# One-column products behind the spread of a root, AV beside the following transposes, and embedding copies behind the weight casts

## The chip, the cores and the metric

The kernel runs on one core of a Trainium2 chip. The core has a matmul engine (TensorE, PE in the profile, with its weight loads shown apart as PEld), three engines for elementwise work (VectorE = DVE, ScalarE = ACT, GpSimd = POOL) and a queue engine that issues DMAs (SyncE = SP). Matmul results land in PSUM, which has eight banks; all else lies in SBUF. The metric is the device time of one execution in microseconds.

## The reference, cut to what matters

A two-layer encoder trunk over 256 positions, width 2048, all in float32:

```python
for i in range(2):
    hn = rmsnorm(h, norm_g[i])
    a_val, a_glu, a_z, q, k, v, b_z = split(hn @ w_in[i])
    ya = conformer_conv(a_val, a_glu, ...)          # GLU, 31 taps, LayerNorm over channels, SiLU
    ya = ya * silu(a_z)
    yb = window_attention(q, k, v, bias, sink) * silu(b_z)   # 16 heads of 64, 4 key heads
    h = h + concat([ya, yb]) @ w_out[i]
    e = rmsnorm(p[i] @ w_pe[i], pe_g[i])
    h = h + e * sigmoid(h @ w_pg[i])
out = rmsnorm(h, final_g)
```

## The kernel before

Activations lie transposed, channels on the 128 partitions and the 256 positions along the free axis. Every large product is made of three fp32r matmuls of 256 columns (`mm3`, lines 399 to 401): the high part of the weights with the high and the low part of the activations, then the low part of the weights with the high part of the activations. Weights come by DMA in chunks of two halves of 128 x 1024. Each half is cast to its high part by ACT (L168), and DVE subtracts to get the low part (L171; L176 for the first two halves of layer 0). `ahead(h)` issues these splits up to half `h`, and a small pool of five split halves is kept in front of PE.

The order on DVE, PE and ACT is the order of the program text; only POOL's and SP's instructions are placed by the framework. Work beside the main stream is written as generators in a list `side`. `pump()` runs after every weight half (24 matmuls) and advances each generator in the list by one `yield`, in the order in which they were added; `wait(n)` yields n times. The depthwise convolution's taps (DVE, L559) are handed out by the same pump.

The parts that the change touches:

- `rstd_col` (L349) sums squares over channels with one-column products against a tile of ones (L354), each appearing as two PE records, then DVE scales (L359) and POOL raises to the power -0.5 (L361). `rstd_row` (L364) spreads that root over all partitions with two PE transposes of a broadcast column (L368), and ACT copies the row out (L372) unless `copy=False`. There are such pairs for the layer's input norm (`rh0`, `rh1`), for the embedding norm (`re0`, `re1`, in `embed`), for the convolution's LayerNorm (`rv0`, `rv1`, in `lnorm`, where `LY` gives the pumps waited before the sum and before the spread) and for the final norm (`rf`).
- A layer's first products are those of the embedding e = p @ w_pe: eight banks of two tiles each, indexed by `j // 2` (L473 to L509; plain float32 products at L481 in layer 0, `mm3` in layer 1). Among them stand the input norm's sum (at `j // 2 == QQ[l][0]`) and spread (at `QQ[l][1]`), the first splits of the input projection's weights, and the first normalised operands: `operand` multiplies by gain and root on DVE (L453, tile `hn`), ACT casts the high part (L456, tile `hg`) and DVE subtracts the low part (L457). The banks of e are copied out by ACT (L509); in layer 0 the first four wait until `j // 2` is 3, in layer 1 each is copied at once. The first input projection (tiles `ag`) follows, at first two weight halves interleaved.
- `attention` is one generator for each of eight pairs of heads (`i` from 0 to 7): scores on PE (L627, tile `sc`), softmax on DVE and ACT, eight transpose records on PE (L654, tile `pt`), two ACT copies (L658, tile `ptt`), then `wait(2)`, the product with v on PE (L664, tile `av`, eight records of 64 output partitions) and a DVE product with the gate (L667). In steady state one pair starts every four pumps, so PE sees: transposes of one pair, three halves of the projection, AV of that pair with the scores of the pair two later, one half, transposes of the next pair.

The output projection runs its attention half first (`o<-yb`), then its convolution half (`o<-ya`), then the gate product (`g<-h`).

Of the kernel before, what the change touches and what calls it, by code (L numbers as in the profile page):

```python
# [50 lines left out]
NSPL = 5  # L51
SHIFT = 16
MAN = 'DVE,PE,Activation'
LY = (2, 1)
ORD = 1
AW = (0,0,0,0)
NWARM = 6
# [72 lines left out]
def trunk_kernel(ctx: ExitStack, tc: tile.TileContext, xT, pT, wst, par, gain, relb, sinkp, onehot, out):  # L130
    nc = tc.nc
# [105 lines left out]
    def wait(n):  # L237
        for _ in range(n):
            yield
# [66 lines left out]
    ones = cst.tile([P, P], F32, name="ones")  # L306
# [54 lines left out]
        nc.gpsimd.tensor_tensor(col, v, mhalf, ALU.pow)  # L361
        return col

    def rstd_row(col, name, tag="rb", copy=True):  # L364

        bb = bank(name + "b")
        for b in range(2):
            nc.tensor.transpose(bb[:, 0, b * P:(b + 1) * P], col[:, b:b + 1].broadcast_to([P, P]), ident)  # L368
        if not copy:
            return bb[:, 0, :]  # L370
        rb = wk.tile([P, S], F32, name=name + "rb", tag=tag, bufs=1)
        nc.scalar.copy(rb, bb[:, 0, :])  # L372
        return rb

    def fold(a):
        t = wk.tile([P, S], F32, name="fold", tag="sg")
        nc.vector.tensor_add(t, a[:, 0, :], a[:, 1, :])
        return t

    def halves_of(a):  # L380
        return [a[:, 0, :], a[:, 1, :]]
# [54 lines left out]
    hacc = wk.tile([P, 2, S], F32, name="hacc", tag="hacc")  # L436
    for l in range(DEPTH):

        e = halves(bigt(f"e{l}"))
# [23 lines left out]
                    subs.pop(0)()  # L463

        ecopy = []
        for q in range(4):
            n = Cursor.h
            Cursor.h += 1
            if l:
                w = get(n).rearrange("p t (j k c) -> p t j k c", j=4, k=2)  # L470
            else:
                raw = raws[n // 2][:, n % 2, :].rearrange("p (j k c) -> p j k c", j=4, k=2)
            for jj in range(0, 4, 2):  # L473
                j = 4 * q + jj
                b = bank("e")
                for x in range(2):
                    for k in range(2):
                        if l:
                            mm3(b[:, x, :], w[:, :, jj + x, k, :], pp[:, :, k, :], x == 0 and k == 0, k == 1)
                        else:  # L480
                            nc.tensor.matmul(b[:, x, :], raw[:, jj + x, k, :], pf[:, k, :], start=x == 0 and k == 0,  # L481
                                             stop=k == 1, skip_group_check=True)
                if l == 0 and j // 2 < 4:
                    for k in (4 * (j // 2), 4 * (j // 2) + 2):
                        if k < KT - 2:
                            square_acc(hacc, h[k // 8][:, k % 8:k % 8 + 2, :], k == 0, nc.vector)
                    if j // 2 == 3:
                        sq = wk.tile([P, 2, S], F32, name="sq", tag="sq", bufs=3)
                        nc.scalar.activation(sq, h[1][:, 6:8, :], AF.Square)
                        hparts = [fold(hacc)] + halves_of(sq)  # L490
                if j // 2 == QQ[l][0]:
                    dg = rstd_col(hparts, D, f"rh{l}")
                    ahead(4 if l == 0 else Cursor.h - 1 - q + 5)
                if j // 2 == QQ[l][1]:
                    rbs.append(rstd_row(dg, f"rh{l}", copy=False))
                    if l == 0:
                        first_lo(4)
                        ahead(5)
                        operands(0, 1)
                        first_lo(5)  # L500
                        subs.pop(0)()
                        operands(2, 1)
                if QQ[l][1] + (l == 0) <= j // 2 <= QQ[l][1] + 1:
                    operands(4 * (j // 2 - QQ[l][1]), 2)
                ecopy.append((j, b))

                while ecopy and (l or j // 2 >= 3):
                    jc, bc = ecopy.pop(0)
                    nc.scalar.copy(e[jc // 8][:, jc % 8:jc % 8 + 2, :], bc)  # L509
            pump()  # L510
        subs.pop(0)()
        ahead(Cursor.h + 3)
        hsrc = xT if l == 0 else hscr

        def embed(l=l, eacc=eacc, e=e):

            if l == 0:
                yield from wait(8)
                bias_prep()
            for j in range(0, KT, 2):  # L520
                yield from wait(2)
                square_acc(eacc, e[j // 8][:, j % 8:j % 8 + 2, :], j == 0)
            yield from wait(6)
            es = fold(eacc)
            yield from wait(3)
            dg = rstd_col([es], D, f"re{l}")
            yield from wait(2)
            eb = rstd_row(dg, f"re{l}", "reb")
            yield from wait(50)
            while not state["enorm"]:  # L530
                yield
            for j in range(KT):
                d = e[j // 8][:, j % 8, :]
                nc.vector.scalar_tensor_tensor(d, d, pcol(l, PO_PE + j), eb, ALU.mult, ALU.mult)
                yield
# [52 lines left out]
        b = pair(hg, f"k{l}")  # L588
# [23 lines left out]
        def attention(i, qq, after, l=l, v=v, zb=zb):  # L612
            t = i // 4
            yield from wait(after)
            bias = load_bias(i)
            yield
            nm = wk.tile([P, 2, 2], F32, name="nm", tag="nm")
            den = wk.tile([P, 2, 2], F32, name="den", tag="den")
            es = wk.tile([P, 2, 2], F32, name="es", tag="es")
            sk = sinkt[:, l * NQ + 2 * i:l * NQ + 2 * i + 2].unsqueeze(1).broadcast_to([P, 2, 2])  # L620
            each = [(b, hh) for b in range(2) for hh in range(2)]
            o = []
            for b in range(2):
                o.append(bank("sc"))
                for hh in range(2):
                    for x in range(2):
                        nc.tensor.matmul(o[b][:, hh, :], qq[:, hh, b * P:(b + 1) * P], keys[t][x][:, hh, :],  # L627
                                         start=hh == 0 and x == 0, stop=x == 1, skip_group_check=True)
            yield from wait(1 + AW[0])
            s = [wk.tile([P, 2, S], F32, name="s", tag="s", bufs=4) for b in range(2)]  # L630
            for b, hh in each:
                c = l * NQ + 2 * i + hh
                nc.vector.tensor_tensor_reduce(
                    out=s[b][:, hh, :], in0=o[b][:, hh, :], in1=backwards(bias[:, hh, b * P:b * P + S]),
                    scale=1.0, scalar=nsink[:, c:c + 1], op0=ALU.add, op1=ALU.min,
                    accum_out=nm[:, b, hh:hh + 1])
            nc.vector.tensor_add(es, nm, sk)
            yield
            for b, hh in each:
                nc.scalar.activation(s[b][:, hh, :], s[b][:, hh, :], AF.Exp, bias=nm[:, b, hh:hh + 1],  # L640
                                     scale=-1.0, accum_out=den[:, b, hh:hh + 1])
            nc.scalar.activation(es, es, AF.Exp)
            yield from wait(1 + AW[1])
            nc.vector.tensor_add(den, den, es)
            nc.vector.reciprocal(den, den)
            yield from wait(1 + AW[2])
            for b, hh in each:
                nc.scalar.activation(s[b][:, hh, :], s[b][:, hh, :], AF.Copy, scale=den[:, b, hh:hh + 1])
            yield from wait(1 + AW[3])
            o = [bank("pt") for hh in range(2)]  # L650
            for hh in range(2):
                for b in range(2):
                    for kt in range(2):
                        nc.tensor.transpose(o[hh][:, kt, b * P:(b + 1) * P], s[b][:, hh, kt * P:(kt + 1) * P], ident)  # L654
            yield
            pt = [wk.tile([P, 2, S], F32, name="ptt", tag="ptt") for hh in range(2)]
            for hh in range(2):
                nc.scalar.copy(pt[hh], o[hh])  # L658
            yield from wait(2)
            o = bank("av")  # L660
            for kt in range(2):
                for hh in range(2):
                    g = 2 * t + hh
                    nc.tensor.matmul(o[hh * HD:(hh + 1) * HD, 0, :], v[:, kt, g * HD:(g + 1) * HD], pt[hh][:, kt, :],  # L664
                                     start=(kt == 0), stop=(kt == 1))
            yield
            nc.vector.tensor_mul(zb[:, i, :], o[:, 0, :], zb[:, i, :])  # L667
# [31 lines left out]
        def lnorm(l=l, acc=acc, za=za, ya=ya, ysum=ysum, done=done):  # L699
# [15 lines left out]
            yield from wait(LY[0])  # L715
            dg = rstd_col(halves_of(vacc), W_CONV, f"rv{l}")
            yield from wait(LY[1])
            rb = rstd_row(dg, f"rv{l}")
            yield
            for n in range(5):  # L720
                if n < 4:
# [202 lines left out]
```

## Time and profile before

| | us |
|---|---|
| median of three runs | 951.17 |
| lowest and highest run | 944.24, 951.45 |
| the profiled execution | 950.28 |
| its span, first to last instruction | 948.5 |
| PE busy in it | 935.5 (99%) |
| DVE busy | 769.4 (81%) |
| ACT busy | 549.4 (58%) |
| POOL busy | 83.8 (9%) |

The profile is of one execution. Times in it are microseconds from the start of its span. A row of the timeline has the start, the busy time, engine, line, operation and output<-inputs; a bracket at its end gives the engine's idle time before it and what ended that. A row of the windows gives, for a stretch of the span, the busy time and the number of records of each engine that overlap the stretch, the granted PE clock as a share of full speed, the share of the DMA engines in use and the rate in GB/s. PE records overlap, because matmuls are pipelined: the time that a matmul takes from its engine is the distance from its start to the next one's start, not its busy time. DMA moved 192 GB/s on average.

### The profile page before, as it was taken

Reading aid. Unit: us, or ns where it says so; the run is one execution under the profiler, and the core shown is the slowest. Engines: PE = TensorE matmul, PEld = TensorE weight load, DVE = VectorE, ACT = ScalarE, POOL = GpSimd, SP = SyncE. Lnnn points to the kernel's source line nnn. Section 1 sums busy time; section 2 is a strip of 40 time slices with the busy share of each in tenths; the row PEclk is TensorE's granted clock in tenths of the full one; section 3 lists DMA queues with packets and bytes.
Section 4 is the critical chain, followed back from the end, with each engine's and each line's share of the span. In section 5 each row is a group of like instructions: output and inputs, shape, how many; then the busy total and the mean of one; then the engine's idle time right before and its main releaser. Section 6 shows DMA issues by size and latency. Waiting matters only on the chain.

```text
span 948.5 us, 19102 instructions
## 1 busy us (share of the span) xinstructions
PE 935.5 (99%) x7952; PEld 918.8 (97%) x7952; DVE 769.4 (81%) x1290; ACT 549.4 (58%) x830; POOL 83.8 (9%) x79
## 2 busy tenths in 40 slices
PE   8999999999999999999999999999999999999995
PEld 7999999999999999999999999999999999999995
DVE  3899999998887676776679998999888878677663
ACT  4655455787875554454466444558787555546551
POOL 0022001010000000011103200000100010000111
PEclk9999999999999999999999999999999999999998
DMA  8674556555456465556555566465454564655532
GB/s 294 226 254 157 200 178 244 195 188 191 168 174 231 171 224 183 178 179 225 189 196 198 174 219 206 154 217 199 167 205 144 190 223 146 246 186 178 191 121 90
DMA packets 29011, 182.55 MB, mean 192 GB/s; under 512 B 3595, under 2 KB 4156, under 8 KB 9084
## 3 DMA queue, kind: packets, MB, share of 16 engines
q1 hardware_dynamic: 24284, 165.70, 49.9%
q0 software_dynamic: 3344, 12.88, 4.2%
q10 hardware_dynamic: 1296, 2.75, 0.8%
q8 instruction: 62, 1.02, 0.4%
q14 instruction: 25, 0.20, 0.1%
HBM read 177.09 MB, written 4.23 MB: 191 GB/s over the span
## 4 chain that ended last, share of the span: by engine, by line
PE 95%; DVE 3%; DMA 1%; issue 0%; ACT 0%; POOL 0%; ACTq 0%; DVEq 0%
PE g L401 6%; PE g L399 6%; PE g L400 6%; PE ag L401 6%; PE ag L399 6%; PE ag L400 6%; PE o L400 6%; PE o L399 6%; PE o L401 6%; PE za L399 3%; PE zb L400 3%; PE za L400 3%; PE zb L401 3%; PE zb L399 3%; PE q L399 3%; PE za L401 3%
## 5 line engine op out<-in xcount | busy, mean ns | idle before, releaser
L171 DVE TENSOR_TENSOR w<-raw,w 128x1024 fp32r<-128x1024 f32 x306 | 373.2, 1228 | 105.1 <-ACT w L168 104.5
L168 ACT CAST w<-raw 128x1024 fp32r<-128x1024 f32 x308 | 316.2, 1046 | 166.3 <-PE ag L401 40.6
L559 DVE SCALAR_TENSOR_TENSOR cz<-az,pars,cz 128x241 f32<-128x241 f32 (+11 forms) x480 | 217.8, 502 | 1.0
L401 PE MATMUL ag<-hg,w 128*128 128x256 f32 x512 | 143.0, 279 | 0.6 <-DVE w L171 0.5
L399 PE MATMUL ag<-hg,w 128*128 128x256 f32 x512 | 142.8, 279 | 0.0
L401 PE MATMUL g<-h,w 128*128 128x256 f32 x512 | 142.6, 279 | 0.0
L399 PE MATMUL g<-h,w 128*128 128x256 f32 x512 | 142.6, 278 | 0.0
L400 PE MATMUL g<-h,w 128*128 128x256 f32 x512 | 142.6, 278 | 0.0
L400 PE MATMUL ag<-hg,w 128*128 128x256 f32 x512 | 142.5, 278 | 0.0
L401 PEld LDWEIGHTS ag<-hg,w 128*128 128x128 f32 x512 | 96.2, 188 | 1.2 <-DVE w L171 1.0
L401 PEld LDWEIGHTS g<-h,w 128*128 128x128 f32 x512 | 97.2, 190 | 0.0
L400 PEld LDWEIGHTS ag<-hg,w 128*128 128x128 f32 x512 | 96.9, 189 | 0.1
L399 PEld LDWEIGHTS ag<-hg,w 128*128 128x128 f32 x512 | 96.1, 188 | 0.9 <-ACT w L168 0.8
L399 PEld LDWEIGHTS g<-h,w 128*128 128x128 f32 x512 | 96.1, 188 | 0.0
L400 PEld LDWEIGHTS g<-h,w 128*128 128x128 f32 x512 | 96.1, 188 | 0.0
L399 PE MATMUL o<-yb,w 128*128 128x256 f32 x256 | 72.2, 282 | 0.0
L399 PE MATMUL za<-hg,w 128*128 128x256 f32 x256 | 72.0, 281 | 0.0
L400 PE MATMUL o<-yb,w 128*128 128x256 f32 x256 | 71.6, 280 | 0.0
L399 PE MATMUL q<-hg,w 128*128 128x256 f32 x256 | 71.5, 279 | 0.0
L401 PE MATMUL o<-yb,w 128*128 128x256 f32 x256 | 71.4, 279 | 0.0
L399 PE MATMUL zb<-hg,w 128*128 128x256 f32 x256 | 71.4, 279 | 0.0
L399 PE MATMUL o<-ya,w 128*128 128x256 f32 x256 | 71.3, 278 | 0.0
(219 smaller groups left out, 2269.4 us busy)
## 6 DMA issues: line engine op xcount, KB each, us to landing
raw<-in_wst SPq DMA_DIRECT2D x153, 1024.0 KB, 4.9
bias<-fscr POOLq DMA_DIRECT2D x16, 384.0 KB, 4.0
raw<-in_wst SPq DMA_DIRECT2D x4, 512.0 KB, 8.0
az<-in_xT POOLq DMA_DIRECT2D x4, 512.0 KB, 5.3
hscr<-e POOLq DMA_DIRECT2D x2, 1024.0 KB, 5.5
az<-hscr POOLq DMA_DIRECT2D x4, 512.0 KB, 5.8
x<-in_xT SPq DMA_DIRECT2D x3, 512.0 KB, 8.2
out_t<-og ACTq DMA_DIRECT2D x4, 256.0 KB, 3.0
```

The lines of the kernel that those rows point to most:

```text
L168: nc.scalar.copy(hi, raw)
L171: nc.vector.tensor_sub(lo, raw, hi.bitcast(F32))
L399: nc.tensor.matmul(o, w[:, 0], x[:, 0], start=start, stop=False, skip_group_check=True)
L400: nc.tensor.matmul(o, w[:, 0], x[:, 1], start=False, stop=False, skip_group_check=True)
L401: nc.tensor.matmul(o, w[:, 1], x[:, 0], start=False, stop=stop, skip_group_check=True)
L559: nc.vector.scalar_tensor_tensor(acc[:, t, lo_:hi_], a[:, t, lo_ + s:hi_ + s], w(k), acc[:, t, lo_:hi_], ALU.mult, ALU.add)
```

## The change

Four edits.

1. `rstd_row` gets a parameter `settle`. Behind its two transposes it issues that many one-column float32 products of the tile of ones with one of its columns, into the unused second half of the same bank. `embed` and `lnorm` pass `settle=2`; the input norm's and the final norm's spreads do not.
2. `LY` goes from (2, 1) to (2, 2): the spread of the LayerNorm's root is issued one pump later.
3. In `attention` AV waits three pumps behind the copies in place of two, which puts it in the same pump as the transposes of the next pair and ahead of them; the last pair (`i == 7`) waits one.
4. In a layer's first products the sum of squares of layer 0 takes the two halves of the last squares first and the folded sum last; layer 0 issues the second weight half's cast together with the first (`ahead(5)` at the sum, none at the spread); the copies of e begin at `j // 2 == 4` in layer 0, and in both layers those of `j // 2` 6 and 7 are issued after the casts that follow the loop.

```diff
-LY = (2, 1)
+LY = (2, 2)
...
-    def rstd_row(col, name, tag="rb", copy=True):
+    def rstd_row(col, name, tag="rb", copy=True, settle=0):
...
+        for b in range(settle):
+            nc.tensor.matmul(bb[:, 1, b:b + 1], ones, ones[:, 0:1], start=True, stop=True, skip_group_check=True)
         if not copy:
...
+        def copied(j, b, e=e):
+            nc.scalar.copy(e[j // 8][:, j % 8:j % 8 + 2, :], b)
...
-                        hparts = [fold(hacc)] + halves_of(sq)
+                        hparts = halves_of(sq) + [fold(hacc)]
                 if j // 2 == QQ[l][0]:
                     dg = rstd_col(hparts, D, f"rh{l}")
-                    ahead(4 if l == 0 else Cursor.h - 1 - q + 5)
+                    ahead(5 if l == 0 else Cursor.h - 1 - q + 5)
                 if j // 2 == QQ[l][1]:
                     rbs.append(rstd_row(dg, f"rh{l}", copy=False))
                     if l == 0:
                         first_lo(4)
-                        ahead(5)
                         operands(0, 1)
...
-                while ecopy and (l or j // 2 >= 3):
-                    jc, bc = ecopy.pop(0)
-                    nc.scalar.copy(e[jc // 8][:, jc % 8:jc % 8 + 2, :], bc)
+                while ecopy and 4 * (l == 0) <= j // 2 < 6:
+                    copied(*ecopy.pop(0))
             pump()
         subs.pop(0)()
         ahead(Cursor.h + 3)
+        for c in ecopy:
+            copied(*c)
...
-            eb = rstd_row(dg, f"re{l}", "reb")
+            eb = rstd_row(dg, f"re{l}", "reb", settle=2)
...
-            yield from wait(2)
+            yield from wait(1 if i == 7 else 3)
             o = bank("av")
...
-            rb = rstd_row(dg, f"rv{l}")
+            rb = rstd_row(dg, f"rv{l}", settle=2)
```

## The prediction

> **What bounds the kernel now.** I read the page first, its span and its chain.
>
> ```profile
> span 948.5 us, 19102 instructions
> PE 95%; DVE 3%; DMA 1%; issue 0%; ACT 0%; POOL 0%; ACTq 0%; DVEq 0%
> ```
>
> TensorE (PE) carries 95% of the chain, so the time is the sum of its matmul starts. What can change is how many records it runs, the microseconds in which it stands, and the pace of its stream. The pace is read from windows of pure fp32r products. A record lasts 0.28 us and a new one starts every 0.11 us, so about two are already running when a window opens; the pace is the window divided by its PE count less two.
>
> ```profile
> 53.10:118.30 65.20, 65.20 (x578) 65.20 (x577) 65.09 (x105) 32.24 (x40) 14.95 (x11) 1.00 0.59 205
> 126.00:137.00 11.00, 11.00 (x96) 11.00 (x95) 10.59 (x22) 7.34 (x14) 0.00 (x0) 1.00 0.41 144
> 137.40:164.10 26.70, 26.70 (x238) 26.70 (x237) 25.93 (x45) 12.99 (x16) 3.33 (x3) 1.00 0.68 238
> 312.70:480.40 167.70, 167.70 (x1426) 167.70 (x1426) 116.01 (x138) 82.74 (x102) 8.95 (x8) 1.00 0.55 194
> 500.60:561.60 61.00, 61.00 (x520) 61.00 (x519) 59.65 (x92) 32.66 (x42) 13.99 (x7) 1.00 0.58 195
> 569.50:600.60 31.10, 31.10 (x277) 31.10 (x276) 28.27 (x53) 15.53 (x22) 0.00 (x0) 1.00 0.49 170
> 601.00:628.70 27.70, 27.70 (x238) 27.70 (x237) 26.56 (x46) 13.81 (x17) 3.31 (x3) 1.00 0.69 237
> 777.60:934.80 157.20, 157.20 (x1390) 157.20 (x1389) 107.07 (x131) 81.95 (x107) 7.76 (x6) 1.00 0.47 168
> ```
>
> The columns are the stretch, PE, PEld, DVE, ACT and POOL busy with counts, granted clock, DMA share and GB/s. The same matmul runs at two paces with PE never idle: 65.20/576 = 113.2 ns, 113.1 from 137.40, 113.1 from 569.50 and 157.20/1388 = 113.3; but 117.0 from 126.00, 167.70/1424 = 117.8, 61.00/518 = 117.8, and 117.4 from 601.00. A pace holds for a hundred microseconds and more. The granted clock is 1.00 in all eight rows, so the gate is not it. The row from 53.10 holds the fast pace with DVE busy for 65.09 of its 65.20 us, and the one from 777.60 runs the same lines as the slow one from 312.70; so neither a full DVE nor the work itself sets the pace. It is left behind by whatever stood before the stretch. 312.70 begins behind the spread of rv0 (two transposes), 126.00 behind that of re0.
>
> **The change: products behind a spread.** `settle=2` puts two one-column products behind the transposes of re0, re1, rv0 and rv1, four PE records each.
>
> ```profile
> 119.50 0.28 PE L401 MATMUL k<-hg,w 128*128 128x256 f32 x1
> 119.61 0.50 PE L354 MATMUL re0c<-ones,fold 128*128 128x1 f32 x4
> 119.98 0.37 PE L399 MATMUL k<-hg,w 128*128 128x256 f32 x1
> ```
>
> Four such records push the next product from 119.61 to 119.98; I take 0.4 us for each spread, and the restart behind them is paid behind the transposes already. Four spreads: +1.6 us. A sentence of the Trainium skill (TensorE: Matmul & The Clock Gate, Back-to-back issue gap) puts a product of 1 to 64 columns at about 60 cycles; by it the sixteen records would be about 0.4 us, an estimate. The row says four times that, and the row is used. The copies of eb and rb on ACT may wait 0.4 us longer; eb is first used 50 pumps later and rb only for the ya half of the output projection, so nothing is late. What the products buy is the pace behind them:
>
> ```profile
> 309.38 0.28 PE L401 MATMUL o<-yb,w 128*128 128x256 f32 x1
> ...
> 311.76 0.28 PE L401 MATMUL o<-yb,w 128*128 128x256 f32 x1
> 312.12 0.43 PE L368 MATMUL rv0b<-ident,rv0col 128*128 128x128 f32 x2
> 312.31 0.36 PE L399 MATMUL o<-yb,w 128*128 128x256 f32 x1
> ```
>
> ```profile
> 120.60:125.30 4.70, 4.70 (x44) 4.70 (x44) 4.70 (x10) 1.31 (x2) 0.89 (x1) 1.00 0.49 160
> 563.80:567.60 3.80, 3.80 (x36) 3.80 (x35) 3.76 (x10) 1.05 (x1) 1.39 (x2) 1.00 0.70 239
> 191.10:193.60 2.50, 2.50 (x24) 2.50 (x23) 2.46 (x7) 2.00 (x5) 0.00 (x0) 1.00 0.03 13
> 219.00:221.60 2.60, 2.60 (x24) 2.60 (x24) 2.60 (x6) 2.12 (x4) 0.00 (x0) 1.00 0.00 0
> ```
>
> Behind the one-column products of rv0 21 products take 2.38 us (113 ns), and the two windows behind those of re0 and re1 give 112: fast in all three, where the spreads left 117.0 (re0), 117.8 (rv0), 113.1 (re1) and 113.3 (rv1). So I take fast behind every settled spread. rv0: 1424 products by 4.5 ns, -6.4 us. re0: 94 by 4 ns, -0.4. re1 and rv1 are fast already: 0. One risk lies behind re0: at 600.6, where v gives way to zb, layer 1 fell from fast to slow without a stall, while layer 0 rose there. If that step turns the pace over, layer 0's 236 products from 137.40 become slow: +1.0, which I take; without it 0.
>
> **LY (2, 2).** The spread of rv comes one weight half later. In the rows above PE starts it 0.36 us after the product before, where a product starts after 0.11: 0.25 us of waiting for POOL's power. 24 products (2.7 us) cover that. Layer 1 is taken alike, an estimate: -0.5. DVE and ACT work behind it moves 2.7 us, and the ya half is some forty microseconds away.
>
> **AV next to the transposes.** Heads 0 to 6 run AV with the following head's transposes instead of ahead of the scores.
>
> ```profile
> 164.14 0.28 PE L401 MATMUL zb<-hg,w 128*128 128x256 f32 x1
> ...
> 165.22 0.28 PE L399 MATMUL zb<-hg,w 128*128 128x256 f32 x1
> ```
>
> ```profile
> 179.68 0.28 PE L401 MATMUL q<-hg,w 128*128 128x256 f32 x1
> 179.79 1.03 PE L654 MATMUL pt<-ident,s 128*128 128x128 f32 x8
> 180.59 0.37 PE L399 MATMUL q<-hg,w 128*128 128x256 f32 x1
> ```
>
> ```profile
> 188.73 0.28 PE L401 MATMUL zb<-hg,w 128*128 128x256 f32 x1
> 188.94 1.08 PE L664 MATMUL av<-ptt,v 128*64 128x256 f32 x8
> 189.95 0.39 PE L627 MATMUL sc<-keys0h,qq 128*128 128x256 f32 x1
> ...
> 191.01 0.28 PE L399 MATMUL zb<-hg,w 128*128 128x256 f32 x1
> ```
>
> From product to product, AV with scores costs 2.28 us, transposes 0.91, scores alone 1.08. AV with transposes is not shown: 1.22 (188.73 to 189.95) and 0.80 (179.79 to 180.59) make 2.02 if the change from AV to transposes costs what that to scores does, 1.92 if it costs nothing, which are the ends. A round goes from 3.19 to 3.10: -0.09, six rounds a layer, and head 6, whose AV stood alone at 1.22, saves 0.11: -1.3 in all. The 24 products behind the scores also ran slow in some rounds (the two last windows above: 24 records in 2.60 against 2.50 us); with no AV ahead they should keep the fast pace of the transposes: half of twelve by 0.1, -0.6. Together -1.9; ends -0.5 and -3.3. The copies out of PSUM and the DVE product after AV move a step, with ACT and DVE otherwise in the same order; POOL's bias loads depend on the scores, not on AV.
>
> **First products.** Layer 0 issues the second cast (`ahead(5)`) at once, puts five copies of e behind both casts, takes the ready squares before the fold, and puts the last two copies behind the casts of the next weights; layer 1 does only the last.
>
> ```profile
> 17.13 0.60 PE L354 MATMUL rh0c<-ones,fold 128*128 128x1 f32 x4 [1.54 <-DVE fold L377]
> ```
>
> ```profile
> 26.84 1.06 ACT L509 COPY e<-e 128x512 f32<-128x512 f32 x2
> 27.80 1.06 ACT L168 CAST w<-raw 128x1024 fp32r<-128x1024 f32 x1
> ```
>
> ```profile
> 31.30 0.19 PEld L401 LDWEIGHTS ag<-hg,w 128*128 128x128 f32 x1 [0.72 <-DVE w L171]
> ```
>
> ```profile
> 489.62 1.56 ACT L509 COPY e<-e 128x512 f32<-128x512 f32 x3
> 491.06 1.07 ACT L168 CAST w<-raw 128x1024 fp32r<-128x1024 f32 x1
> 500.14 0.39 PE L401 MATMUL ag<-hg,w 128*128 128x256 f32 x1
> ```
>
> At 31.30 PE had waited 0.72 us for DVE's low half, which follows ACT's casts, which stood behind 1.06 us of copies. Without these the halves come a microsecond earlier. The reordered sum starts PE up to 0.5 us earlier, but the five copies then stand ahead of the first hg cast and give most of that back. I take -1.2; ends -0.3 and -1.6. What is late next is DVE's following pair, in step with PE. The copies are hidden by PE's stream; if a bank were needed before its copy, PE would wait one copy, 0.5 us, but eight banks are in turn. SP loads the same chunk at the same place.
>
> In layer 1 the casts start 1.0 us earlier (two of the three copies move), so the late low half at 500.14 is in time: its restart (500.14 is 0.02 late, and the next product costs a further 0.1 us) and one taken alike in the pair before, an estimate, -0.3. The slow 61 us begin at this very stall; unbroken, the stream keeps the fast pace, which layer 0 held over the same loop from 53.10: 518 by 4.5 ns, -2.3.
>
> **Sum.** -6.4 - 0.4 + 1.0 + 1.6 - 0.5 - 1.9 - 1.2 - 0.3 - 2.3 = -10.4. The profiled execution took 950.28 us (948.5 of span and 1.8 around it), 0.9 under the median of 951.17; so 939.9.
>
> **Rivals.** (a) Layer 1's stretch from 500.6 goes slow at another small stall, as it did from 601 with none: 942.2. (b) The products do not set the pace; three cases are few, and rv1 went fast without them. rv0 and re0 keep theirs: 939.9 + 6.4 + 0.4 - 1.0 = 945.7. (c) AV ahead of the transposes leaves the slow pace for all 96 products of a round: fourteen by 0.43 us, 945.9; against it speaks that the fast row from 777.60 stands right behind two transposes. (d) The other side, slower than before: the products with `ones` as weights, not a data tile as in the rows, leave the slow pace. Then (b), and rv1's 1388 products turn slow (+6.3) and re1's 275 (+1.2): 953.2. It decides as soon as the 157 us of layer 1 are slow. (e) There is one pace and no state: all pace terms go, leaving +1.6 - 0.5 - 1.3 - 1.2 - 0.3 = -1.7: 948.6. This is also what the Trainium skill's rule would make of it (same page and section: N/2.4 + 2.5 ns on a warm array, one figure for one width). By that rule 256 columns take 109.2 ns whatever came before; the trace disagrees, with 113.3 and 117.8 at the same clock.
>
> **Chances.** Main case 0.50, (a) 0.18, (b) 0.18, (c) 0.06, (d) 0.04, (e) 0.04. The prediction is the main case, 939.9; its own range, from the ends above and the +1.0, is 937 to 942. With (a), (b) and (c) the range is 937.0 to 946.3. A measurement of this kernel tells about 1%, 9.5 us, from no change, so faster means under 941.7: nearly all of the main case and a third of (a), 0.54. (b), (c), (e) and the rest lie within 1%: 0.44; 0.02 is left for slower by over 1%, since (d) itself ends within it.
>
> **What would show it.** Right: the windows behind rv0's spread and behind 500 at 113 ns, no 0.36 us before the spreads of rv, no wait for DVE at 30 us, rounds of AV and transposes near 2.0 us, scores 1.1. Wrong: a long window at 118 behind a settled spread, v to zb fast in layer 0, PE waiting for e's copies, or the time of before at 944.24, its lowest run, turning out to be the same pace won by luck.

## The result, and the profile after

| | before | after |
|---|---|---|
| median of 12 runs, us | 949.94 | 942.61 |
| lowest and highest, us | 943.73, 951.45 | 941.75, 943.53 |
| the profiled execution, us | 950.28 | 943.05 |

The ratio of the means is 0.9933, 95% interval 0.9915 to 0.9951: 0.7% faster, clear of the noise, but within the 1% that the prediction didn't count as faster and to which it gave 0.44. The forecast of 939.9 was 2.7 us too low. The main case's own range (937 to 942) missed the time by 0.6 us; the wide range with three of the rivals (937.0 to 946.3) held it. Not only the median fell: the runs of before spread over 7.7 us, those of after over 1.8.

The page of the changed kernel, its span, busy times and chain:

```profile
span 941.3 us, 19132 instructions
...
PE 928.9 (99%) x7968; PEld 912.3 (97%) x7968; DVE 767.9 (82%) x1290; ACT 550.3 (58%) x830; POOL 83.0 (9%) x79
...
PE 95%; DVE 2%; DMA 1%; ACT 1%; issue 0%; ACTq 0%; DVEq 0%
```

PE carries the same 95% of the chain; the time is still the sum of its starts. The windows of the changed kernel over six of the stretches that the prediction showed (columns as there; the pace is the window divided by the PE count less two):

```profile
125.50:136.30 10.80, 10.80 (x94) 10.80 (x93) 10.16 (x20) 7.05 (x13) 0.00 (x0) 1.00 0.34 126
136.60:163.50 26.90, 26.90 (x240) 26.90 (x239) 26.14 (x45) 13.28 (x17) 3.32 (x3) 1.00 0.68 235
316.20:474.90 158.70, 158.70 (x1403) 158.70 (x1402) 114.15 (x136) 81.58 (x101) 8.96 (x8) 1.00 0.56 197
492.50:553.40 60.90, 60.90 (x539) 60.90 (x539) 59.05 (x90) 32.75 (x43) 11.60 (x7) 1.00 0.54 191
593.50:621.00 27.50, 27.50 (x236) 27.50 (x235) 26.36 (x45) 13.61 (x16) 3.30 (x3) 1.00 0.70 245
773.20:928.00 154.80, 154.80 (x1369) 154.80 (x1367) 105.50 (x129) 80.72 (x105) 7.76 (x6) 1.00 0.46 165
```

The two large changes are there: behind the spread of rv0, 158.70/1401 = 113.3 ns where it was 117.8, and in layer 1's first products, 60.90/537 = 113.4 where it was 117.8. Two things did not happen. Behind re0 the pace is still slow, 10.80/92 = 117.4, although that spread now has its one-column products; and at 136.60, where v gives way to zb, layer 0 still rises to 113.0.

The spread of rv0 on PE, in the timeline of the changed kernel:

```profile
315.04 0.28 PE L403 MATMUL o<-yb,w 128*128 128x256 f32 x1
315.15 0.38 PE L368 MATMUL rv0b<-ident,rv0col 128*128 128x128 f32 x2
315.37 0.50 PE L370 MATMUL rv0b<-ones 128*128 128x1 f32 x4
315.73 0.36 PE L401 MATMUL o<-yb,w 128*128 128x256 f32 x1
```

The transposes start 0.11 us behind the product, so POOL's root is no longer waited for. From the last product to the next there are 0.69 us. Before it was 0.55, of which 0.25 was the wait: by that the one-column products cost 0.39. Experiment 3 below has the same spread without them and without a wait, and there it is 0.25 (314.72 to 314.97): by that they cost 0.44.

And AV beside the transposes, in a round of layer 0's attention, on the same kernel's timeline:

```profile
192.44 0.28 PE L403 MATMUL zb<-hg,w 128*128 128x256 f32 x1
192.64 1.08 PE L670 MATMUL av<-ptt,v 128*64 128x256 f32 x8
193.66 1.09 PE L660 MATMUL pt<-ident,s 128*128 128x128 f32 x8
194.51 0.37 PE L401 MATMUL zb<-hg,w 128*128 128x256 f32 x1
```

The block takes 2.07 us from product to product; 2.02 was forecast. But look at the products behind four such blocks in turn (windows of the changed kernel, each between one block and the next scores):

```profile
195.00:202.60 7.60, 7.60 (x67) 7.60 (x66) 7.24 (x22) 6.89 (x16) 0.70 (x1) 1.00 0.71 263
209.30:216.90 7.60, 7.60 (x69) 7.60 (x69) 3.62 (x6) 6.79 (x16) 1.71 (x1) 1.00 0.58 192
223.20:230.80 7.60, 7.60 (x67) 7.60 (x66) 7.43 (x21) 7.37 (x17) 1.53 (x2) 1.00 0.77 259
237.50:245.10 7.60, 7.60 (x70) 7.60 (x69) 3.91 (x7) 6.80 (x15) 0.00 (x0) 1.00 0.58 189
```

116.9, 113.4, 116.9 and 111.8 ns (one record more or less in such a short window is 1.7 ns; by the starts of the single products the second and the fourth run alike). Each block turns the pace over: what came in fast leaves slow, what came in slow leaves fast. It does so at all fourteen blocks of the two layers. Every second round runs 96 products at the slow pace, 0.43 us (48 behind the last block of each layer).

### The profile page after: what moved, and what is told of

It is laid out like the page before. It is cut to its first block, busy times and chain, and to the rows that moved or that the text cites. A ratio compares the mean times of both kernels' runs of the same rounds, so it can differ in the third digit from the quotient of the medians.

```text
span 941.3 us, 19132 instructions
## 1 busy us (share of the span) xinstructions
PE 928.9 (99%) x7968; PEld 912.3 (97%) x7968; DVE 767.9 (82%) x1290; ACT 550.3 (58%) x830; POOL 83.0 (9%) x79
## 4 chain that ended last, share of the span: by engine, by line
PE 95%; DVE 2%; DMA 1%; ACT 1%; issue 0%; ACTq 0%; DVEq 0%
PE o L401 6%; PE o L402 6%; PE o L403 6%; PE ag L401 6%; PE g L403 6%; PE ag L403 6%; PE ag L402 6%; PE g L402 6%; PE g L401 6%; PE za L401 3%; PE za L403 3%; PE za L402 3%; PE zb L401 3%; PE zb L403 3%; PE zb L402 3%; PE q L401 3%
## 5 line engine op out<-in xcount | busy, mean ns | idle before, releaser
L401 PE MATMUL q<-hg,w 128*128 128x256 f32 x256 | 71.9, 281 | 0.0
L401 PE MATMUL o<-yb,w 128*128 128x256 f32 x256 | 71.9, 281 | 0.0
L402 PE MATMUL q<-hg,w 128*128 128x256 f32 x256 | 71.4, 279 | 0.0
L403 PE MATMUL q<-hg,w 128*128 128x256 f32 x256 | 71.4, 279 | 0.0
L402 PE MATMUL o<-yb,w 128*128 128x256 f32 x256 | 71.3, 278 | 0.0
```

The source lines that it names most:

```text
L401: nc.tensor.matmul(o, w[:, 0], x[:, 0], start=start, stop=False, skip_group_check=True)
L402: nc.tensor.matmul(o, w[:, 0], x[:, 1], start=False, stop=False, skip_group_check=True)
L403: nc.tensor.matmul(o, w[:, 1], x[:, 0], start=False, stop=stop, skip_group_check=True)
```

## The experiments

Three theories were set against each other for the 168 us behind rv0. The prediction's: the one-column products behind the transposes set the pace. A rival: the place in the program does, since `LY` moves the spread by 24 products. Another: the wait does. Before, PE stood for POOL's root at this spread, and with `LY` (2, 2) it doesn't. In the diffs the kernel that the edit starts from is named. Ratios are against runs of before on the same chip.

**1. Products alone.** Before, with products behind the spreads of rv only and `LY` (2, 1):

```diff
-            rb = rstd_row(dg, f"rv{l}")
+            rb = rstd_row(dg, f"rv{l}", settle=2)
```

> The kernel before with the two one-column products behind the spread of rv alone, at its old place (LY 2, 1). Theory A, the products set the fast pace behind a spread: the 168 us behind rv0 run at 113.3 ns in every execution, 6.3 us less, for two times 0.45 us of products: 944.5 against a median of 949.9, and the spread of the runs shrinks. Rival B, the pace behind a spread is left by the moment at which it falls, and the products have no part in it: rv0 stays at 117.8 ns in most executions, 950.8.

Measured: 950.39 us, ratio 0.9991 (0.9949 to 1.0033). The spread on its timeline, and its windows behind rv0, at the first products of layer 1, and behind rv1:

```profile
313.00 0.28 PE L403 MATMUL o<-yb,w 128*128 128x256 f32 x1
313.37 0.43 PE L368 MATMUL rv0b<-ident,rv0col 128*128 128x128 f32 x2
```

```profile
314.50:482.30 167.80, 167.80 (x1427) 167.80 (x1427) 115.93 (x137) 82.72 (x102) 8.95 (x8) 1.00 0.54 194
502.20:563.30 61.10, 61.10 (x522) 61.10 (x520) 59.76 (x92) 32.66 (x42) 12.46 (x7) 1.00 0.56 195
779.90:936.70 156.80, 156.80 (x1385) 156.80 (x1385) 107.07 (x130) 81.68 (x106) 7.75 (x6) 1.00 0.47 168
```

The products are there, the wait is there (0.37 us from product to transpose, where 0.11 is the rule), and the stretch behind rv0 is slow: 167.80/1425 = 117.8. So the products don't buy the pace. The ten runs lie in three groups, four from 943.97 to 945.02, four from 950.18 to 953.36, and two at 956.21 and 957.64; the means of the groups are 7.0 and 5.3 us apart, near the 6.4 of one long stretch at the other pace, which suggests that either layer's can come out either way, though only the middle group has a trace.

**2. The later spread alone.** Before, with this line only:

```diff
-LY = (2, 1)
+LY = (2, 2)
```

> The kernel before with LY (2, 2) alone: the spread of rv one weight half later, no products. Theory A: the pace behind rv0 stays slow (117.8 ns); only the wait of 0.25 us per layer goes, 949.4. Rival B: the later place is what makes the stretch fast, 943.1.

Measured: 942.89 us, ratio 0.9915 (0.9876 to 0.9954). The same three stretches:

```profile
317.00:475.70 158.70, 158.70 (x1403) 158.70 (x1402) 114.14 (x136) 81.57 (x101) 8.96 (x8) 1.00 0.55 198
496.00:554.40 58.40, 58.40 (x517) 58.37 (x516) 57.27 (x87) 32.64 (x42) 10.96 (x7) 1.00 0.57 199
773.00:928.00 155.00, 155.00 (x1371) 155.00 (x1369) 105.46 (x129) 80.83 (x107) 7.76 (x6) 1.00 0.46 165
```

113.3 behind rv0, without a single one-column product. One figure has brought the time of the whole change. Something not looked for stands in the second row: layer 1's first products run at 58.40/515 = 113.4 too, although this kernel keeps the late low halves there, as the timeline of the same kernel shows. The product of 495.19 starts 0.14 us behind the one before it, and the next one 0.22 behind that:

```profile
495.05 0.28 PE L400 MATMUL ag<-hg,w 128*128 128x256 f32 x1
495.19 0.39 PE L401 MATMUL ag<-hg,w 128*128 128x256 f32 x1
495.41 0.28 PE L399 MATMUL ag<-hg,w 128*128 128x256 f32 x1
```

So a product that had to be waited for left the fast pace here (at three places in this trace: 489.62, 495.19 and 500.75), and the slow one in the two kernels above. Even there not each did: in the kernel before the first such product, at 494.57, left the fast pace (46 spacings from 494.80 to 500.01, 113.3 ns), and only the second, at 500.14, the slow one. Of five runs of this kernel four lie from 942.74 to 943.06 and one at 945.70; the gap of 2.7 is about what this stretch is worth, but no trace shows that run.

**3. The whole change without its products.** After, with `settle` taken out of `embed` and `lnorm`:

```diff
-            eb = rstd_row(dg, f"re{l}", "reb", settle=2)
+            eb = rstd_row(dg, f"re{l}", "reb")
...
-            rb = rstd_row(dg, f"rv{l}", settle=2)
+            rb = rstd_row(dg, f"rv{l}")
```

> The changed kernel without any of the products behind the spreads, all else kept. Theory A: the 158 us behind rv0 fall back to 117.8 ns (+6.2 us) and sixteen records go (-1.8 us): 947.0, with runs spread over several us as before. Rival B: the stretch stays fast and the records are saved: 940.8.

Measured: 941.52 us, ratio 0.9908 (0.9882 to 0.9934), span 939.6. Its windows behind re0, rv0 and rv1:

```profile
125.10:135.90 10.80, 10.80 (x94) 10.80 (x93) 10.39 (x21) 7.15 (x14) 0.00 (x0) 1.00 0.42 146
315.50:474.30 158.80, 158.80 (x1404) 158.80 (x1402) 114.12 (x136) 81.73 (x101) 8.97 (x8) 1.00 0.56 198
771.60:926.00 154.40, 154.40 (x1364) 154.40 (x1364) 105.46 (x129) 80.66 (x106) 7.76 (x6) 1.00 0.46 166
```

The paces are 117.4, 113.3 and 113.4, within 0.2 ns those of the changed kernel. The products change nothing behind them, and cost the difference of the spans: 941.3 - 939.6 = 1.7 us, 0.4 for each spread.

**4. AV back at its old place.** After, with:

```diff
-            yield from wait(1 if i == 7 else 3)
+            yield from wait(2)
```

> The changed kernel with AV back at its old place, two pumps behind the copies for all heads. Theory A2, AV ahead of the transposes turns the pace over each round, so that every second round runs 72 to 96 products at 118 ns: without it all stretches behind transposes are fast again and the time falls by 1.5 us, to 941.1. Rival B2, the slow rounds were an accident of this execution and the block of AV with transposes saves 0.1 us a round as forecast: 942.6 to 944.5.

Measured: 941.66 us, ratio 0.9906 (0.988 to 0.9932), span 940.0 against 941.3. The first of the windows that were slow in the changed kernel:

```profile
195.00:202.00 7.00, 7.00 (x64) 7.00 (x63) 6.34 (x18) 6.68 (x15) 0.70 (x1) 1.00 0.70 236
```

7.00/62 = 112.9 instead of 116.9. With AV back ahead of the scores the 72 products behind the transposes are fast in every round; 24 products behind AV and scores still run slow in some rounds, the same rounds in all ten traces with AV at this place. Beside the transposes it loses 1.3 us by the spans of one execution each; the intervals of the two ratios overlap.

**5. The first products alone.** Before, with edit 4 of the change only (shown in part) and `LY` (2, 1):

```diff
-                while ecopy and (l or j // 2 >= 3):
+                while ecopy and 4 * (l == 0) <= j // 2 < 6:
...
+        for c in ecopy:
+            copied(*c)
```

> The kernel before with the edit of a layer's first products alone: LY (2, 1), so PE again waits 0.25 us for POOL before each spread of rv; AV at its old place; no products. Theory C, a spread that PE has to wait for leaves either pace, by chance of the moment, and one that it does not wait for leaves the fast one: times in two groups, around 946.5 (rv0 slow) and 940.2 (rv0 fast); layer 1's ag stretch fast in all, without its stalls. Rival: ag stays slow in the trace although its stalls are gone, so that the copies are worth 1 us only: 949.0 and 942.7.

Measured: 947.05 us, ratio 0.9957 (0.9942 to 0.9972). Behind rv0, and in layer 1's first products:

```profile
311.70:479.50 167.80, 167.80 (x1427) 167.80 (x1427) 115.90 (x137) 82.83 (x102) 8.96 (x8) 1.00 0.54 194
495.80:557.70 61.90, 61.90 (x549) 61.90 (x547) 60.06 (x91) 33.85 (x44) 11.55 (x7) 1.00 0.55 192
```

With the wait at rv0 kept (it is longer here, 0.84 us from product to transpose), that stretch is slow again, 117.8. Two groups of times were expected, around 946.5 and 940.2; all four runs lie in the upper one. With the copies behind the casts the low halves come in time, and layer 1's stretch is fast, 61.90/547 = 113.2. The first products bring their part without the other edits.

**6. The two parts that pay, without the two that don't.** Experiment 5 with `LY` (2, 2): no products, AV at its old place.

> The kernel before with LY (2, 2) and the edit of the first products, nothing else. Theory C: no stall before the spreads of rv and none in layer 1's first products, so both long stretches fast, no AV rounds at the slow pace and no sixteen records: 940.1, below the changed kernel by 2.5 us, in one narrow group. Rival: one of the two stretches is slow without the products or AV's move: 942.4 or 946.4.

Measured: 939.39 us (938.88 to 939.80), ratio 0.9878 (0.9862 to 0.9895), faster than both kernels. Behind rv0 and rv1:

```profile
313.80:472.60 158.80, 158.80 (x1404) 158.80 (x1402) 114.12 (x136) 81.68 (x101) 8.97 (x8) 1.00 0.55 198
...
768.90:924.00 155.10, 155.10 (x1372) 155.10 (x1370) 105.47 (x129) 80.92 (x107) 7.76 (x6) 1.00 0.47 167
```

158.80/1402 = 113.3 and 155.10/1370 = 113.2: both stretches are fast.

**7. Products where a stretch is slow without a wait.** In experiment 6 layer 1's first zb weights start a slow stretch of 27 us, as in every other kernel. Two one-column products go into `pair`, behind the first weight half of zb, amid fp32r products:

```diff
-    def pair(X, name):
+    def pair(X, name, reset=False):
...
+            if reset and x == 0:
+                rs = bank("reset")
+                for c in range(2):
+                    nc.tensor.matmul(rs[:, 0, c:c + 1], ones, ones[:, 0:1], start=True, stop=True, skip_group_check=True)
...
-            b = pair(hg, f"zb{l}_{i}")
+            b = pair(hg, f"zb{l}_{i}", reset=l == 1 and i == 0)
```

> As e6_place_first, with two one-column products put into layer 1's stream behind the first weight half of zb, where the traces show it slow for 27 us from v's end on. Theory D, one-column products between two runs of fp32r products leave the fast pace, as all sums of squares do: the 214 products behind them at 113.3 ns, 1.0 us less, for 0.45 us: 939.6, and the window of zb fast in the trace. Rival: they leave what they find, as behind re0's spread: still 117.8 ns and 940.6.

Measured: 939.01 us, ratio 0.9872 (0.9858 to 0.9887). Experiment 6's window of that stretch, and then this kernel's:

```profile
592.00:619.50 27.50, 27.50 (x236) 27.50 (x235) 26.36 (x46) 14.12 (x16) 3.31 (x3) 1.00 0.65 236
```

```profile
593.90:618.90 25.00, 25.00 (x222) 25.00 (x221) 23.86 (x40) 12.62 (x16) 3.31 (x3) 1.00 0.64 226
```

117.5 became 113.6. One-column products that stand between fp32r products left the fast pace here, as the prediction read from the sums; behind transposes they left what the transposes left. The gain, some 215 products by 4 ns, less 0.4 for the products, is too small for these times to tell from experiment 6.

**8. Before once more,** one execution with a profile, unedited.

> The kernel before, looked at once more. Theory C: the 168 us behind rv0 are slow or fast by chance while the program is the same; if the execution takes about 944 the trace shows them at 113.3 ns, if about 950 at 117.8. Rival: the executions at 944 differ elsewhere (the granted clock, layer 1's ag stretch), with rv0 at 117.8 ns at either time.

Measured: 952.29 us. Behind rv0, in layer 1's first products, and behind rv1:

```profile
316.00:480.00 164.00, 164.00 (x1395) 164.00 (x1394) 115.85 (x137) 79.64 (x97) 8.39 (x7) 1.00 0.54 191
504.00:562.00 58.00, 58.00 (x495) 58.00 (x494) 56.56 (x86) 31.36 (x41) 12.43 (x7) 1.00 0.56 197
780.00:934.00 154.00, 154.00 (x1362) 154.00 (x1361) 106.59 (x129) 81.52 (x106) 7.76 (x6) 1.00 0.48 171
```

117.7, 117.6 and 113.2: the same three paces as in the first profile of it. The wait before the spread of rv0 is 0.84 us here against 0.36 there, from product to transpose, and leaves the slow pace too.

But at another place the two traces of this one kernel differ. The third step of layer 0's output projection needs a low half of `yb` from DVE, and PE has just to wait for it: the weight load of that product starts 0.20 us behind the one before it, where 0.11 is the rule. DVE's row in the first profile (the first of the three ends at 294.78, the load starts at 294.84), and the window behind that product up to the sum of rv0; then the same window in this second profile:

```profile
294.09 1.90 DVE L739 TENSOR_TENSOR yb<-az,yb 128x512 fp32r<-128x512 f32 x3 [1.06 <-ACT yb L738]
295.10:308.20 13.10, 13.10 (x113) 13.10 (x113) 10.33 (x14) 7.50 (x10) 1.03 (x2) 1.00 0.62 223
```

```profile
297.10:309.70 12.60, 12.60 (x113) 12.60 (x112) 9.82 (x14) 7.39 (x10) 0.99 (x2) 1.00 0.64 225
```

13.10/111 = 118.0 and 12.60/111 = 113.5. One program, one place, the same short wait, and either pace behind it.

**9. The spread at its old pump, its wait moved.** Experiment 6 with the sum one pump earlier, so that the spread stands where it stood before but the root is ready:

```diff
-LY = (2, 2)
+LY = (1, 2)
```

> As e6_place_first with LY (1, 2): the spread of rv stands at the place it had before (three pumps after the squares), but its sum is issued a pump earlier, so PE should not wait for POOL at the spread (at most 0.3 us at the sum instead, for the last square). Theory C1, the wait in front of the spread is what leaves the slow pace: rv0's stretch fast in every execution, 939.4 to 940.0. Theory C2, the place in the stream decides: rv0 slow, 945.7.

Measured: 940.95 us, ratio 0.9927 (0.99 to 0.9954), but the ten runs fall in two groups, three from 946.53 to 947.97 and seven from 939.88 to 941.47. The profiled execution is of the upper group. The wait did not go; the sum now waits for DVE:

```profile
304.70 1.02 PE L354 MATMUL rv0c<-ones,vacc 128*128 128x1 f32 x8 [0.64 <-DVE vacc L392]
```

The windows behind the sum and behind the spread in layer 0, then the same in layer 1:

```profile
305.90:311.00 5.10, 5.10 (x46) 5.10 (x45) 4.49 (x6) 1.80 (x2) 0.72 (x1) 1.00 0.41 153
311.90:480.00 168.10, 168.10 (x1431) 168.10 (x1429) 116.28 (x138) 83.13 (x103) 8.97 (x8) 1.00 0.55 194
768.60:773.20 4.60, 4.60 (x43) 4.60 (x42) 4.09 (x6) 1.66 (x2) 0.71 (x1) 1.00 0.45 146
774.40:931.00 156.60, 156.60 (x1384) 156.60 (x1384) 107.23 (x131) 81.79 (x107) 7.75 (x6) 1.00 0.48 169
```

In layer 0 the waited-for sum leaves the slow pace: the window gives 5.10/44 = 115.9, in which one record is 2.6 ns, and the 45 spacings from the start at 305.90 to that at 311.20 are 117.8 each. The spread behind it, for which nothing waits, keeps that pace, 117.6 for 168 us; in layer 1 the same program with the same wait leaves 112.2 and then 113.3. Here the spread stands at its old place with no wait of its own, and the time of one program still falls in two groups, 6.5 us apart by their means, near 1424 products by 4.5 ns. If these are the two paces of a stretch, the place alone can't be what decides, since it is the same in both groups. That the lower group is the one with a fast stretch is inferred from the gap; no trace is of it.

**10. The spread at the new pump, with a wait.** Experiment 6 with the sum a pump later:

```diff
-LY = (2, 2)
+LY = (3, 1)
```

> As e6_place_first with LY (3, 1): the spread of rv stands at the changed kernel's place (four pumps after the squares), but its sum is a pump later too, so PE waits about 0.25 us for POOL again. Theory C1: some executions slow behind rv0 or rv1, so 945.9 (or 952 with both), or two groups of times; at the least the first spacings behind the spreads differ between layers, which they do not without the wait. Theory C2: both stretches fast, 939.9 in one group.

Measured: 939.01 us (938.70 to 939.42), ratio 0.9889 (0.9859 to 0.9919). The intended wait did not occur, because POOL had the root in time:

```profile
311.17 0.71 POOL L361 TENSOR_TENSOR rv0col<-rv0v,mhalf 128x2 f32<-128x2 f32 x1 [15.50 <-DVE rv0v L359]
```

So this is one more kernel without a wait, and both its long stretches are fast. It doesn't test the place against the wait.

**What they say together.** Behind rv0 the trace is fast in all seven kernels in which PE waits neither at the sum nor at the spread (after, 2, 3, 4, 6, 7, 10), and slow in all five traces with such a wait (before, 1, 5, 8, 9). Products, AV and the first products may be as they like. In layer 1's first products it is fast in all eight traces without a late low half (after, 3 to 7, 9, 10), slow in three with one and fast in one (2); of the eight such products in these four traces three left the slow pace. Where nothing is waited for, a changeover at a given place left the same pace in every trace for the same pace ahead of it: re0 leaves slow with and without products, an AV block beside transposes turns the pace over, a sum leaves fast. A spread that isn't waited for, and behind which the same products go on, keeps the pace that it finds: fast behind fast, and slow behind slow in experiment 9. Where PE waits, either pace is left: fast behind rv1 in all five traces that wait there, slow behind rv0 in all five. The short wait for `yb` occurs in both layers of all twelve traces, and left the slow pace 17 times and the fast one 7 times. The steady runs of the kernels without waits at rv fit (spreads of 0.9 us in experiment 6, 0.7 in 7 and 10), as do the wide ones with them (7.7 in before, 13.7 in experiment 1), though experiment 5's four runs, with a wait, spread by 1.5 only.

What stays open: what the two paces are in the array, and what about a wait decides between them. That waiting for the root left slow behind rv0 and fast behind rv1 each time is not explained. `LY` (2, 2) takes the wait away and moves the spread at once, and no trace parts the two at rv0: a wait at the new place was meant by experiment 10, and the old place with no wait at all by experiment 9, and neither was obtained. That the wait does it and not the place rests on the other waits, above all on that for `yb`, which left both paces in one program.

## Why the prediction was right and wrong

| term | predicted, us | measured, us | read from |
|---|---|---|---|
| rv0's stretch to the fast pace | -6.4 | -6.4 | windows; experiments 1, 2 |
| re0's stretch to the fast pace | -0.4 | 0 | window at 125.50 |
| v to zb in layer 0 falls to slow | +1.0 | 0 | window at 136.60 |
| one-column products | +1.6 | +1.7 | span less experiment 3's |
| waits for POOL's root | -0.5 | -0.5 | none left in the trace |
| AV beside the transposes | -1.9 | +1.5 | attention in the two traces |
| layer 0's first products | -1.2 | -1.0 | start of the 401st fp32r product, 72.46 to 71.44 (the second with a slower clock at the start, see the end) |
| layer 1's restarts and its stretch | -2.6 | -2.6 | window at 492.50; experiment 5 |
| sum | -10.4 | -7.3 | profiled executions: -7.2 |

- **The step that failed** is "What the products buy is the pace behind them", from which it followed: "So I take fast behind every settled spread." Its size came true by another edit. Experiment 1 has the products and the slow stretch, experiment 2 the fast stretch without products, and experiment 3 shows nothing lost without them. The edit that was priced at 0.5 us for its wait brought 6.4 more; with it the wait went, behind which the pace had been slow. The rival that denied the products their effect, (b), was right in that and wrong in its time, since it too gave the wait no part in the pace. A hint had been in the quoted rows: two of the slow stretches began at the wait of 312.12 and at the stall of 500.14. The second was named as the cause, the first was not. It was no more than a hint, since the stretch behind rv1 began at such a wait as well and was fast.
- That the wide range held the time is luck to this extent: the largest term came from an edit to which it was not given. The rival nearest to 942.6 is (a) with 942.2, and its stall did not come, since layer 1's stretch is fast. What parts the forecast from the result is the term of AV.
- The same step gave the terms of re0 and of zb. Both fell with it: -0.4 and +1.0 were 0.6 too much together.
- **AV** is the term with the largest error, 3.4 us. The block was sized well (2.02 against 2.07 us). What failed is "with no AV ahead they should keep the fast pace of the transposes": the block turns the pace over. The rival in which it leaves every round slow, 14 by 0.43 us, was half true; every second round is slow. Experiment 4 takes it back.
- The first products, the waits for the root and layer 1's stretch came as worked out. The mechanism of the last, that a stretch goes slow at the stall, holds with the addition that a stall may leave either pace: three of eight left the slow one.

## What to carry to other kernels

When a stream of equal matmuls runs at two paces, look at what stands at the start of each slow stretch, and first of all for a wait of the matmul engine there, however short: 0.25 us at one spread cost 6.4 us behind it. Cover the wait with work that is there already before adding instructions to reset anything, and judge each edit alone: here two of four edits brought everything, and leaving out the other two was worth 3 us. A wide spread of the times of one kernel can be a hint that some such wait decides by chance.

## What the runs showed of the hardware that was not expected

- Two paces of the same product, 113.3 and 117.8 ns at a granted clock of 1.00. One stretch holds its pace over 1424 products, through the changes from the output projection to the gate product and to the next embedding.
- A one-column product costs about 0.2 us on PE's path (0.39 to 0.45 us for two).
- In some executions PE runs at a lower granted clock from 19 to 23 us. The windows of that time in the changed kernel and, behind it, in before:

```profile
19.00:23.00 4.00, 4.00 (x14) 3.03 (x13) 2.62 (x5) 3.08 (x7) 0.79 (x1) 0.57 0.40 162
```

```profile
19.00:23.00 4.00, 4.00 (x21) 3.50 (x20) 3.50 (x5) 2.42 (x4) 0.61 (x1) 1.00 0.44 180
```

Fourteen records against 21 in the same 4 us, at 0.57 and 1.00 of the clock. Kernels of either kind show it (experiments 1, 2, 4 and 8 too), so it is no part of the change. What it costs differs with edit 4. The 401st fp32r product starts at 72.46 in the first profile of before, without it, and at 73.70 to 74.42 in the three kernels with the same first products that have it (experiments 1, 2 and 8). With edit 4 it starts at 71.44 and 71.68 with it (the changed kernel, experiment 4) and at 70.99 to 71.46 in the six kernels without it. So some 2 us of the spread of before's times can come from this clock and not from the paces, and edit 4 takes most of that away as well. The Trainium skill (TensorE: Matmul & The Clock Gate, What's actually happening) says that the window of activity by which the clock is set runs freely and isn't reset when a kernel starts, so that the moment of a change of clock varies. That the clock differs from execution to execution agrees with these rows; what the window is no run here shows.
